# Joining two loads and two stores of a fused RMSNorm-GELU kernel into 64 KB pieces, and gamma into one transfer

## The chip, the cores and the metric

The kernel runs on one core of a Trainium2 chip. The metric is device time in microseconds (us) for one execution, lower is better. A run's profile has its own span, from the first to the last instruction, 1.7 to 2.1 us shorter than the time.

## The reference, cut to what matters

```python
# x: (8, 1024, 2048) float32, gamma: (2048,), eps: 1e-5
rms = np.sqrt(np.mean(x ** 2, axis=-1, keepdims=True) + eps)
out = gamma * x / rms
return 0.5 * out * (1 + np.tanh(np.sqrt(2 / np.pi) * (out + 0.044715 * out ** 3)))
```

x is 67.11 MB and so is the result. Each is moved once.

## The kernel before

The 8192 rows are cut into 16 groups of 512 rows. A group fills one slot: 128 partitions with 4 consecutive rows of 8 KB each, so one partition of a group is a run of 32 KB in memory. There are six slots. Loads are issued by SP ("SPq" in the profile), stores by ACT ("ACTq"). Each is one transfer, except that store 0 is cut into a 64 KB head and the rest.

```python
ROWS = 4; SLOTS = 6; GW = 64; CHUNK = 1024; NARROW = 128
x3 = x.rearrange("b s d -> (b s) d").rearrange("(g p r) d -> g p r d", p=P, r=R)
slot = [sbuf.tile([P, R, D], FP32, name=f"slot{i}") for i in range(SLOTS)]
flat_pieces = {0: [(0, NARROW), (NARROW, R * D)]}

def load(g):
    nc.sync.dma_start(out=slot[g % SLOTS], in_=x3[g])

def gelu_store(g):
    ...                                    # four gelu activations on ACT
    for a, b in flat_pieces.get(g, [(0, R * D)]):
        nc.scalar.dma_start(out=dst[:, a:b], in_=flat[:, a:b])

for k in range(0, D, CHUNK):               # gamma in two transfers
    nc.scalar.dma_start(out=gamma_row[...], in_=gamma[k : k + CHUNK]...)
for g in range(SLOTS):
    load(g)
...                                        # gamma is spread to 128 partitions by matmuls
for g in range(G + 1):
    if g < G:
        squares(...)                       # ACT, 2 or 3 of the 4 rows
        squares_on_vector(...)             # DVE, the others
        inverse_rms(g); scale(g, 0, R)     # DVE, one step on POOL
    if g:
        gelu_store(g - 1)
        if g - 1 + SLOTS < G:
            load(g - 1 + SLOTS)            # waits until store g-1 has left the slot
```

A transfer reports its landing on one of eight completion counters. The build hands these out in turn (not quite in program order: in the changed kernel gamma has counter 0 and load 0 counter 1), so that the eighth transfer gets counter 7 and the ninth counter 0 again.

## Time and profile before

| | before |
|---|---|
| time, first three runs | 317.41 us (317.17 to 317.51) |
| span of the profiled run | 315.3 us |
| busiest compute engines | ACT 66%, DVE 63% |
| DMA, 72 to 300 us | share 1.00, 433 GB/s |
| transfers | 2 gamma + 16 loads + 17 stores = 35 |

The prediction below walks through the page. One part of it that the prediction uses only in numbers is the list of DMA issues (tile, issuer, how many, size of each, median us from issue to landing):

```profile
slot<-in_x_dram SPq DMA_DIRECT2D x16, 4096.0 KB, 31.4
out_dram<-slot ACTq DMA_DIRECT2D x15, 4096.0 KB, 50.0
out_dram<-slot ACTq DMA_DIRECT2D x1, 4032.0 KB, 27.3
out_dram<-slot ACTq DMA_DIRECT2D x1, 64.0 KB, 13.2
```

A 4 MB transfer at 433 GB/s takes 9.7 us alone. That a store takes 50 us to land says that it mostly stands in line.

### The profile page before, as it was taken

The page shows a single profiled execution, that of the slowest core. Times are in us where ns is not written, and L with a number is a line of the kernel's source. Part 1 is how long each engine was busy: PE and PEld are TensorE (multiplying, and loading weights), DVE is VectorE, ACT ScalarE, POOL GpSimd, SP SyncE. Part 2 cuts the span into 40 slices and gives each one's busy share as a digit, 9 for nine tenths or more (in the row PEclk, how much of TensorE's full clock was granted, in tenths as well). Part 3 has the DMA queues.
Part 4 walks back from the last instruction along what each step waited for, and adds up shares of the span by engine and source line. Part 5 has one row for each costly group of instructions (what it writes and reads, how often), then busy time and mean ns, then how long its engine had stood idle before and what let it go on. Part 6 is the DMA issues. An engine that isn't in the chain of part 4 may idle for free.

```text
span 315.3 us, 463 instructions
## 1 busy us (share of the span) xinstructions
PE 7.2 (2%) x8; PEld 2.5 (1%) x8; DVE 198.6 (63%) x129; ACT 207.0 (66%) x150; POOL 16.4 (5%) x21
## 2 busy tenths in 40 slices
PE   0900000000000000000000000000000000000000
PEld 0300000000000000000000000000000000000000
DVE  0089889898988843927687286376934639684000
ACT  1327999999986819569292793948649397499000
POOL 0010110101010101001010010101001010010000
DMA  8999999999999999999999999999999999999996
GB/s 333 412 453 416 452 395 404 461 403 461 417 449 420 442 424 441 420 445 424 441 424 441 428 436 432 432 432 432 432 436 436 428 445 420 453 412 453 412 453 279
DMA packets 4818, 134.24 MB, mean 426 GB/s; under 512 B 592, under 2 KB 720, under 8 KB 720
## 3 DMA queue, kind: packets, MB, share of 16 engines
q1 hardware_dynamic: 2304, 67.11, 49.7%
q10 hardware_dynamic: 2512, 67.12, 49.3%
q14 instruction: 2, 0.02, 0.0%
HBM read 67.12 MB, written 67.11 MB: 426 GB/s over the span
## 4 chain that ended last, share of the span: by engine, by line
another core or an unknown queue 36%; DMA 27%; DVE 16%; ACT 7%; PE 2%; issue 2%; POOL 1%; SPq 1%; ACTq 0%; DVEq 0%; POOLq 0%
DMA out_dram<-slot 14%; DVE slot L109 11%; DMA slot<-in_x_dram 10%; ACT slot L120 7%; DVE spare L82 4%; DMA spare<-in_gamma_dram 2%; PE gamma_ps L142 2%; POOL y L95 1%; SPq L68 1%; ACT junk L72 1%; DVE ms L90 0%; DVE z L98 0%; DVE z L99 0%; DVE rstd L102 0%
## 5 line engine op out<-in xcount | busy, mean ns | idle before, releaser
L109 DVE TENSOR_TENSOR slot<-slot,gamma_ps 128x8192 f32<-128x8192 f32 (+1 forms) x19 | 139.2, 7334 | 0.0
L72 ACT ACTIVATE junk<-slot 128x2048 f32<-128x2048 f32 x42 | 79.0, 1882 | 79.8 <-DMA slot<-in_x_dram 77.4
L120 ACT ACTIVATE slot<-slot,rstd 128x2048 f32<-128x2048 f32 x64 | 122.7, 1987 | 2.8 <-DVE slot L109 2.3
L82 DVE SCALAR_TENSOR_TENSOR spare<-slot 128x2048 f32<-128x2048 f32 x22 | 50.4, 2290 | 43.6 <-DMA slot<-in_x_dram 29.1
L95 POOL TENSOR_TENSOR y<-ms,power 128x4 f32<-128x4 f32 x16 | 16.1, 1007 | 263.1 <-DVE ms L90 263.1
L90 DVE TENSOR_SCALAR ms<-ssq 128x4 f32<-128x4 f32 x16 | 2.7, 170 | 24.2 <-ACT junk L72 22.8
L98 DVE TENSOR_TENSOR z<-ms,y 128x4 f32<-128x4 f32 x16 | 2.6, 164 | 19.0 <-POOL y L95 19.0
L72 ACT ACTIVATION_READ_ACCUMULATOR junk<-slot 128x1 f32 x42 | 7.8, 186 | 0.0
L142 PE MATMUL gamma_ps<-spare,ones 1*128 1x512 f32 x8 | 7.2, 1073 | 8.1 <-DMA spare<-in_gamma_dram 8.1
L102 DVE SCALAR_TENSOR_TENSOR rstd<-z,y 128x4 f32<-128x4 f32 x16 | 2.6, 163 | 0.5
L99 DVE SCALAR_TENSOR_TENSOR z<-z,y 128x4 f32<-128x4 f32 x16 | 2.6, 163 | 0.5
L140 ACT ACT_TABLE_LOAD x1 | 1.3, 1283 | 2.0 <-issue 2.0
L142 PEld LDWEIGHTS gamma_ps<-spare,ones 1*128 1x128 f32 x8 | 2.5, 325 | 11.2 <-issue 10.7
L82 DVE DVE_READ_ACCUMULATOR spare<-slot 128x1 f32 x22 | 1.8, 82 | 0.0
L138 DVE MEMSET warm<- 1x1 f32 x1 | 0.1, 59 | 0.8 <-PEq L181 0.8
L140 ACT ACTIVATE warm<-warm 1x1 f32<-1x1 f32 x1 | 0.2, 202 | 0.0
L139 DVE MEMSET ones<- 1x128 f32 x1 | 0.2, 165 | 0.0
L137 POOL MEMSET power<- 128x4 f32 x1 | 0.1, 101 | 0.3 <-POOLq L181 0.3
L181 POOL MEMSET const-float32-0.0<- 128x1 f32 x1 | 0.1, 98 | 0.2 <-issue 0.2
L181 POOL MEMSET const-bfloat16-1.0<- 128x1 bf16 x1 | 0.1, 102 | 0.0
L181 POOL MEMSET const-uint8-127<- 128x1 uint8 x1 | 0.1, 102 | 0.0
L181 POOL MEMSET const-float32-1.0<- 128x1 f32 x1 | 0.1, 98 | 0.0
## 6 DMA issues: line engine op xcount, KB each, us to landing
slot<-in_x_dram SPq DMA_DIRECT2D x16, 4096.0 KB, 31.4
out_dram<-slot ACTq DMA_DIRECT2D x15, 4096.0 KB, 50.0
out_dram<-slot ACTq DMA_DIRECT2D x1, 4032.0 KB, 27.3
out_dram<-slot ACTq DMA_DIRECT2D x1, 64.0 KB, 13.2
spare<-in_gamma_dram ACTq DMA_DIRECT2D x2, 4.0 KB, 8.2
```

What stands on the lines that cost most here:

```text
L68: nc.sync.dma_start(out=slot[g % SLOTS], in_=x3[g])
L72: nc.scalar.activation(out=junk, in_=slot[g % SLOTS][:, q, :], func=ACT.Square, accum_out=ssq[:, g, q : q + 1],)
L82: nc.vector.scalar_tensor_tensor(out=spare[:, :, 0:GW], in0=row, scalar=1.0, in1=row, op0=ALU.bypass, op1=ALU.mult, accum_out=ssq[:, g, q ...
L90: v.tensor_scalar(out=ms, in0=ssq[:, g, :], scalar1=1.0 / D, scalar2=eps_f, op0=ALU.mult, op1=ALU.add,)
L95: nc.gpsimd.tensor_tensor(out=y_, in0=m_, in1=power, op=ALU.pow)
L98: v.tensor_tensor(out=z_, in0=m_, in1=y_, op=ALU.mult)
L99: v.scalar_tensor_tensor(out=z_, in0=z_, scalar=-0.5, in1=y_, op0=ALU.mult, op1=ALU.mult)
L102: v.scalar_tensor_tensor(out=rstd[:, g, :], in0=z_, scalar=1.5, in1=y_, op0=ALU.add, op1=ALU.mult,)
L109: nc.vector.tensor_tensor(out=rows, in0=rows, in1=gamma_ps.unsqueeze(1).to_broadcast([P, n, D]), op=ALU.mult,)
L120: nc.scalar.activation(out=slot[g % SLOTS][:, r, :], in_=slot[g % SLOTS][:, r, :], func=ACT.Gelu_apprx_tanh, scale=rstd[:, g, r : r + 1],)
L140: nc.scalar.activation(out=warm, in_=warm, func=ACT.Gelu_apprx_tanh)
L142: nc.tensor.matmul(out=gamma_ps[:, k : k + 512], lhsT=ones, rhs=gamma_row[:, k // GW : (k + 512) // GW, 0:GW], start=True, stop=True,)
```

## The change

Its intent is fewer and larger transfers: groups 2 and 3 get 8 consecutive rows per partition and come in one load, 12 and 13 leave in one store, each partition being one run of 64 KB; gamma comes in one transfer. That makes 1 + 15 + 16 = 32 transfers. In the program, gamma's transfer also moves behind the first loads. The core of the diff (cut):

```diff
+LOAD_PAIR = 1
+STORE_PAIR = 6
-GW = 64
-CHUNK = 1024
+GW = 128
+    def pair_part(a, k):
+        n = 2 * R * P
+        return a[k * n : (k + 1) * n].rearrange("(p r) d -> p r d", p=P)
+    def part(a, g):
+        if g // 2 in (LOAD_PAIR, STORE_PAIR):
+            return pair_part(a, g // 2)[:, g % 2 * R : g % 2 * R + R, :]
+        return a[g * R * P : (g + 1) * R * P].rearrange("(p r) d -> p r d", p=P)
...
-    slot = [sbuf.tile([P, R, D], FP32, name=f"slot{i}") for i in range(SLOTS)]
+    pair = [sbuf.tile([P, 2 * R, D], FP32, ...) for i in range(SLOTS // 2)]
+    slot = [pair[i // 2][:, i % 2 * R : i % 2 * R + R, :] for i in range(SLOTS)]
...
+            if g // 2 != STORE_PAIR:
+                nc.scalar.dma_start(out=part(o2, g), in_=slot[g % SLOTS])
+            elif g % 2:
+                nc.scalar.dma_start(
+                    out=pair_part(o2, g // 2), in_=pair[g // 2 % (SLOTS // 2)]
+                )
...
         for g in range(SLOTS):
-            load(g)
+            if g // 2 != LOAD_PAIR:
+                load(g)
+            elif g % 2:
+                nc.sync.dma_start(
+                    out=pair[LOAD_PAIR], in_=pair_part(x2, LOAD_PAIR)
+                )
```

More of the change, by code (lines that the diff above doesn't have):

```diff
@@ L38 @@
     eps_f = float(eps)
-    x3 = x.rearrange("b s d -> (b s) d").rearrange("(g p r) d -> g p r d", p=P, r=R)
-    o3 = out.rearrange("b s d -> (b s) d").rearrange("(g p r) d -> g p r d", p=P, r=R)
-    G = x3.shape[0]
+    x2 = x.rearrange("b s d -> (b s) d")
+    o2 = out.rearrange("b s d -> (b s) d")
+    G = x2.shape[0] // (P * R)
+    def pair_part(a, k):
[5 more added lines that the diff above has]
+        return a[g * R * P : (g + 1) * R * P].rearrange("(p r) d -> p r d", p=P)
     sbuf = ctx.enter_context(tc.tile_pool(name="sbuf", bufs=1))
@@ L46 @@
     )
-    slot = [sbuf.tile([P, R, D], FP32, name=f"slot{i}") for i in range(SLOTS)]
-    spare = sbuf.tile([P, D // GW, GW + 8], FP32, name="spare")
+    pair = [
+        sbuf.tile([P, 2 * R, D], FP32, name=f"pair{i}") for i in range(SLOTS // 2)
+    ]
+    slot = [pair[i // 2][:, i % 2 * R : i % 2 * R + R, :] for i in range(SLOTS)]
+    spare = sbuf.tile([P, D // GW, GW + 16], FP32, name="spare")
     gamma_row = spare[0:1]
@@ L59 @@
     junk = psum.tile([P, D], FP32, name="junk")
-    flat_pieces = {0: [(0, NARROW), (NARROW, R * D)]}
     def on_vector(g):
@@ L67, in load @@
     def load(g):
-        nc.sync.dma_start(out=slot[g % SLOTS], in_=x3[g])
+        nc.sync.dma_start(out=slot[g % SLOTS], in_=part(x2, g))
     def squares(g, r, n):
@@ L114, in scale, with gelu @@
         )
-    def gelu_store(g):
-        flat = slot[g % SLOTS].rearrange("p r d -> p (r d)")
-        dst = o3[g].rearrange("p r d -> p (r d)")
+    def gelu(g):
         for r in range(R):
@@ L125, in gelu_store, with store @@
             )
-        for a, b in flat_pieces.get(g, [(0, R * D)]):
-            nc.scalar.dma_start(out=dst[:, a:b], in_=flat[:, a:b])
-    with tc.manual_schedule():
-        for k in range(0, D, CHUNK):
-            nc.scalar.dma_start(
-                out=gamma_row[:, k // GW : (k + CHUNK) // GW, 0:GW],
-                in_=gamma[k : k + CHUNK].rearrange("(o a b) -> o a b", o=1, b=GW),
-            )
-        for g in range(SLOTS):
-            load(g)
+    def store(g):
+        if g:
+            if g // 2 != STORE_PAIR:
[4 more added lines that the diff above has]
+                )
+            return
+        src = pair[0].rearrange("p r d -> p (r d)")
+        dst = part(o2, 0).rearrange("p r d -> p (r d)")
+        for a, z in ((0, NARROW), (NARROW, R * D)):
+            nc.scalar.dma_start(out=dst[:, a:z], in_=src[:, a:z])
+    with tc.manual_schedule():
+        for g in range(SLOTS):
+            if g // 2 != LOAD_PAIR:
[4 more added lines that the diff above has]
+                )
+        nc.scalar.dma_start(
+            out=gamma_row[:, :, 0:GW],
+            in_=gamma.rearrange("(o a b) -> o a b", o=1, b=GW),
+        )
         nc.gpsimd.memset(power, -0.5)
@@ L161 @@
             if g:
-                gelu_store(g - 1)
+                gelu(g - 1)
+                store(g - 1)
                 if g - 1 + SLOTS < G:
```

## The prediction

> **What bounds the kernel now.** I read the page's engine shares first, then the row of the 40 slices, the table of windows, the waits of the load queue, and last the timeline of the store queue near both ends. The page:
>
> ```profile
> span 315.3 us, 463 instructions
> PE 7.2 (2%) x8; PEld 2.5 (1%) x8; DVE 198.6 (63%) x129; ACT 207.0 (66%) x150; POOL 16.4 (5%) x21
> DMA  8999999999999999999999999999999999999996
> DMA packets 4818, 134.24 MB, mean 426 GB/s; under 512 B 592, under 2 KB 720, under 8 KB 720
> ```
>
> No compute engine is busy more than two thirds of the span, while the DMA row stands at nine tenths from the second slice to the last but one. The 134.24 MB are x read once and the output written once, so no byte can go. How close to a limit the transfers run is seen in windows (start:end, length, five engines' busy time, clock, DMA share, GB/s):
>
> ```profile
> 0.00:5.00 5.00, 0.00 (x0) 0.00 (x0) 0.22 (x2) 1.49 (x2) 0.30 (x5) 1.00 0.75 275
> 2.00:32.00 30.00, 7.16 (x8) 2.48 (x8) 15.32 (x10) 12.92 (x13) 1.01 (x1) 1.00 0.99 426
> 72.00:300.00 228.00, 0.00 (x0) 0.00 (x0) 147.18 (x95) 156.10 (x110) 12.08 (x12) 1.00 1.00 433
> 310.00:315.30 5.30, 0.00 (x0) 0.00 (x0) 0.00 (x0) 0.00 (x0) 0.00 (x0) 1.00 0.47 204
> ```
>
> A DMA share of 1.00 over 228 us at 433 GB/s: the sixteen DMA engines never pause. At 433 GB/s all bytes take 134.24 / 0.433 = 310.0 us. The remaining 5.3 us of the span are its two ends (no byte before 1.5 us; the last leaves at about 312.6 us, its receipt and the program's end take 2.7 us) and a read stage at 426 instead of 433. So **only three things can move the time**: the rate, an emptied queue, or the ends.
>
> The chain of waits puts 36% on "another core or an unknown queue". In order of time these are stretches of 18.9 us between load issues, so I take them for transfer time, as the load queue's own waits say:
>
> ```profile
> SPq L68 <- DMA out_dram<-slot: 223.1, 11, 32.5
> SPq L195 <- DMA out_dram<-slot: 73.4, 1, 73.4
> SPq L68 <- DMA spare<-in_gamma_dram: 5.2, 1, 5.2
> ```
>
> Load g+6 waits until store g has left the slot. Those waits recur every 19.3 us (chain: loads issued at 143.8, 163.2, 182.5 us), and one group's load and store, 8.39 MB, take 8.39 / 0.433 = 19.4 us. The wait is thus the full DMA seen from its issuer.
>
> **What the Trainium skill says.** "DMA: Bandwidth & Descriptors", section "Where 436 GB/s comes from", puts the ceiling of sixteen ports at 435.2 GB/s; the 433 of the trace agrees and leaves 0.5%. Same page, "Why small descriptors are slow (HBM only)": about 3 cycles fixed per packet and 32 B of descriptor data per operation. The trace can't split that, but its 0.5% bounds it. Same page, "Queues, rings and completion order": each engine takes turns between queues packet by packet. The trace fits: the 64 KB store piece (512 B per partition, so 8 packets per engine) took 13.2 us to land beside loads in 32 KB packets, each 32.8 KB / (433/16) = 1.2 us; 8 turns make 9.7 us. Same page, "Anatomy of one DMA": about 2 us fixed per DMA, mostly completion, fitted for the GpSimd path; the queues here are the others, and with several transfers queued nothing of it shows in the 433.
>
> **The change part by part.**
>
> *Fewer transfers.* 35 become 32: 15 loads, 16 stores, 1 gamma. 592 small packets are 35 x 16 completions plus 32 gamma pieces. Afterwards: 32 x 16 = 512, and 16 gamma pieces of 512 B. The two pairs turn 512 pieces of 32 KB into 256 of 64 KB, if nothing splits them. Steady-state loss against 435.2 is 0.5% of 228 us = 1.2 us for 23.5 transfers' worth of bytes, so at most 0.05 us per transfer with all its packets. Three fewer: 0.15 us. The 256 saved packets are 16 per engine; by the page's 3 cycles at its 850 MHz, an estimate of 0.06 us that overlaps with the former. Sum: **0.1 to 0.2 us saved**, 0.05% of the time.
>
> *Gamma in one.* Two issues of 0.60 us on ACT become one; they landed 7.2 to 9.1 us after issue. PE starts its eight matmuls (7.2 us) at 8.08 us when the first lands, and DVE waits for them until 15.3 us. One transfer may start PE within about a microsecond of that either way. This is work that hides: the first full store comes only at 38.3 us, with 25.2 MB of loads queued (58 us). The 5.2 us and 4.7 us in which loads 4 and 5 waited for a transfer counter used by gamma and load 0 fall away (in the build the first five load issues carry no wait), with three loads still queued. Worth 0 us.
>
> *Loads 2 and 3 as one.* Group 2 can't start before both halves are in. At 425 GB/s from 1.8 us, 16.8 MB are through at 41.3 us; load 0 was used 1.2 us after the same reckoning (11.7 against 12.96), so 42.5 us. Before:
>
> ```profile
> 38.28 0.34 ACTq L127 DMA_DIRECT2D out_dram<-slot  x1
> 38.67 1.88 ACT L72 ACTIVATE junk<-slot 128x2048 f32<-128x2048 f32 x1 [0.41 <-ACT slot L120]
> 44.65 7.66 ACT L120 ACTIVATE slot<-slot,rstd 128x2048 f32<-128x2048 f32 x4
> 52.34 0.34 ACTq L127 DMA_DIRECT2D out_dram<-slot  x1
> ```
>
> ACT does the squares of group 2 before the gelu of group 1, so a start at 42.5 instead of 38.67 moves store 1 from 52.3 to **56.2 us** and stores 2 to 4 by the same 4 us. Is the store queue then empty? The main part of store 0 started moving when its 64 KB head had landed (32.6 + 13.2 = 45.8) and landed at 38.28 + 27.3 = 65.6. Now the head first alternates with 64 KB load packets: 3.5 per engine are left at 32.6 us, 2.4 us each, then 4.5 turns of 1.2 us. Done at 46 to 48, so store 0 lands at 66 to 68. Store 1 at 56.2 is still 10 us early; and loads 4 and 5 are queued anyhow. Later, store 5 waited for load 6: store 4 was issued at 93.2, store 5 at 109.1, but the ACT work between is 4.0 + 7.7 us, leaving some 4 us of idle time that absorbs the delay. Worth 0 us at the end.
>
> *Stores 12 and 13 as one.* Store 12 now leaves with store 13:
>
> ```profile
> 246.91 0.34 ACTq L127 DMA_DIRECT2D out_dram<-slot  x1
> 266.24 0.34 ACTq L127 DMA_DIRECT2D out_dram<-slot  x1
> 283.58 0.34 ACTq L127 DMA_DIRECT2D out_dram<-slot  x1
> 291.73 0.34 ACTq L127 DMA_DIRECT2D out_dram<-slot  x1
> ```
>
> These are stores 12 to 15. Store 12 goes out 19.3 us later. Store 9 landed at 240.5 (it released load 15), store 10 by the 19.4 us rhythm at 259.9. Store 11 then shares with load 15 until that lands at 271.9 (12 us at half rate, 2.6 MB) and needs (4.2 - 2.6) / 0.433 = 3.7 us more: 275.6 us. The pair at 266.2 is queued **9 us before it is needed**. It then takes 19.4 us, to 295, and stores 14 and 15 (283.6, 291.7) are both queued by then. No slot waits for stores 12 and 13, as no load follows. Worth 0 us.
>
> Sum: 317.41 - 0.15, about **317.2 us**.
>
> **The rivals.** (1) *The queue runs dry.* For it: two joined transfers hold back work for 4 and 19 us. Against it: margins of 10 and 9 us, and a load beside each. Should the end lag by all it could, say the pair leaving 12 us later, it would cost 3 us: about 320. (2) *64 KB pieces run at another rate.* They are 16.8 of 134.2 MB. 10% slower would cost 16.8 / 0.433 x 0.1 = 3.9 us, 321. Nothing in the profile shows a piece of that size, so I can't exclude it, but 32 KB pieces already reach 433 of 435.2, so faster gains little. (3) *The per-transfer cost is larger than bounded here*, because the read stage at 426 hides some: 7 GB/s over 30 us is 0.5 us for three loads, or 0.16 us each, so three fewer give 0.5 us: 316.9. (4) *Turns between queues become unequal*: a 64 KB packet against 32 KB ones takes two thirds. It only shifts bytes between directions, and the pair store meets no load after 275.6 us. 317.2.
>
> **Range and chances.** The three runs before span 0.34 us. I add half a microsecond either way for another phase of reads against writes, and a little on the slow side for rivals 1 and 2: 316.5 to 318.3. Faster by over 2% would be 311.1 us; with all bytes at the page's 435.2 GB/s (308.5 us) and ends of 1.5 and 2.7 us plus the 2.1 us between span and time, it is 314.8, so hardly possible: 1%. Slower by over 2% is 323.8, which takes a rate loss of a sixth in the 64 KB pieces or an idle DMA of 6 us: 3%.
>
> **What would show it.** DMA row still nines; 433 in the middle; packets 4498 with 512 under 512 B (4754 if pieces are split); store 1 near 56 us; load 6 at 66 to 68 us; the pair store near 266 us; last issue near 292 us; last bytes near 312.5. A slice under nine tenths after 40 or after 266 us would speak for rival 1; fewer GB/s around 22 to 42 or 276 to 295 us for rival 2.

## The result, and the profile after

Six runs of the changed kernel have a median of **316.95 us** (316.77 to 317.22), six of the kernel before 317.46 us (317.17 to 317.75). The ratio is 0.9985, with a 95% interval from 0.9972 to 0.9998. The change is worth half a microsecond by the medians: within 2%, and just clear of no change at all, since the interval allows 0.06 to 0.9 us.

The page of the changed kernel:

```profile
span 315.1 us, 457 instructions
...
DMA  8999989999999999999999999999999999999896
...
DMA packets 4498, 134.24 MB, mean 426 GB/s; under 512 B 512, under 2 KB 656, under 8 KB 656
```

The packet counts are the ones worked out ahead (4498 and 512), so the 64 KB pieces go whole. Two slices of the DMA row stand at 8, at 39 to 47 and 292 to 299 us. The prediction had named such slices as the sign of an emptied queue, so they must be read with care. The windows (start:end, length, busy time of five engines, clock, DMA share, GB/s) over the first of them, and the long middle:

```profile
22.00:42.00 20.00, 0.00 (x0) 0.00 (x0) 18.64 (x9) 13.68 (x10) 1.01 (x1) 1.00 1.00 434
32.00:52.00 20.00, 0.00 (x0) 0.00 (x0) 14.89 (x14) 16.21 (x13) 2.02 (x2) 1.00 0.93 386
...
72.00:300.00 228.00, 0.00 (x0) 0.00 (x0) 149.64 (x96) 158.88 (x114) 12.08 (x12) 1.00 1.00 434
...
1.50:2.00 0.50, 0.00 (x0) 0.00 (x0) 0.00 (x0) 0.50 (x1) 0.00 (x0) 1.00 2.99 786
```

The second of these stretches before the change:

```profile
32.00:52.00 20.00, 0.00 (x0) 0.00 (x0) 17.28 (x14) 19.52 (x14) 2.02 (x2) 1.00 0.99 412
```

The line from 1.50 to 2.00 us gives it away: no engine can be busy 2.99 times over. The view books a packet, with all its time and bytes, at the moment it starts. A 64 KB piece lasts 2.4 us and sixteen of them start together, so a slice can lack a whole row of them. When I spread each packet record of the trace over its own duration, every stretch of 10 us from 10 to 310 us is busy to 1.00, in both kernels. The eights are bookkeeping; nothing idles. The windows from 22 to 42 and from 276 to 295 us, which the prediction had named for rival 2, read 434 and 426 GB/s (433 and 428 before); spread in the same way both move 434, so the 64 KB pieces are no slower.

The DMA issues: single loads, the rest and the head of store 0, gamma, and the two joined transfers (8 MB, printed without a size):

```profile
pair<-in_x_dram SPq DMA_DIRECT2D x14, 4096.0 KB, 25.5
...
out_dram<-pair ACTq DMA_DIRECT2D x1, 4032.0 KB, 31.3
out_dram<-pair ACTq DMA_DIRECT2D x1, 64.0 KB, 17.6
spare<-in_gamma_dram ACTq DMA_DIRECT2D x1, 8.0 KB, 7.4
pair<-in_x_dram SPq DMA_DIRECT2D x1, 40.5
out_dram<-pair ACTq DMA_DIRECT2D x1, 30.9
```

And the timeline of ACT: the first squares of group 2, store 1, the joined store, the last store.

```profile
42.16 1.88 ACT L87 ACTIVATE junk<-pair 128x2048 f32<-128x2048 f32 x1 [3.72 <-DMA pair<-in_x_dram]
...
55.83 0.34 ACTq L143 DMA_DIRECT2D out_dram<-pair  x1
...
264.01 0.34 ACTq L145 DMA_DIRECT2D out_dram<-pair  x1
...
289.38 0.34 ACTq L143 DMA_DIRECT2D out_dram<-pair  x1
```

ACT now waits 3.72 us for the joined load, and store 1 leaves at 55.8 instead of 52.3 us. The joined store is issued at 264.0 us and lands 30.9 us later, at 294.9. As its 8.39 MB take 19.4 us, it began to move at about 275.5 us: it stood in line for 11 us.

The remaining difference is at the very end. The load queue's last waits are those of the program's end (source line 195 before, 225 after). Before, one wait of 73.4 us, shown in the prediction; after:

```profile
SPq L225 <- DMA out_dram<-pair: 44.5, 4, 19.3
SPq L225 <- DMA pair<-in_x_dram: 25.1, 1, 25.1
```

Before, the end sits in one wait until everything has landed. After, it moves from one landing to the next, and only the last is left when the last bytes land. Why that is worth time is told with the last experiment.

### The profile page after: what moved, and what is told of

Its sections match the earlier page's. It is cut to its first block, busy times and chain, and to the rows that moved or that the text cites. A ratio compares the mean times of both kernels' runs of the same rounds, so it can differ in the third digit from the quotient of the medians. Undisturbed runs are those within 1.5% of the kernel's fastest.

```text
span 315.1 us, 457 instructions
## 1 busy us (share of the span) xinstructions
PE 7.2 (2%) x8; PEld 2.5 (1%) x8; DVE 198.5 (63%) x129; ACT 206.9 (66%) x150; POOL 16.4 (5%) x21
## 2 busy tenths in 40 slices
DMA packets 4498, 134.24 MB, mean 426 GB/s; under 512 B 512, under 2 KB 656, under 8 KB 656
## 3 DMA queue, kind: packets, MB, share of 16 engines
q10 hardware_dynamic: 2336, 67.12, 49.3%
## 4 chain that ended last, share of the span: by engine, by line
another core or an unknown queue 36%; DMA 36%; ACT 18%; issue 1%; SPq 1%; ACTq 0%
DMA pair<-in_x_dram 21%; DMA out_dram<-pair 15%; ACT pair L133 12%; ACT junk L87 6%; SPq L83 1%; ACTq L143 0%
## 5 line engine op out<-in xcount | busy, mean ns | idle before, releaser
L124 DVE TENSOR_TENSOR pair<-pair,gamma_ps 128x8192 f32<-128x8192 f32 (+1 forms) x19 | 139.2, 7334 | 0.0
L87 ACT ACTIVATE junk<-pair 128x2048 f32<-128x2048 f32 x42 | 79.0, 1881 | 78.7 <-DMA pair<-in_x_dram 76.2
L133 ACT ACTIVATE pair<-pair,rstd 128x2048 f32<-128x2048 f32 x64 | 122.6, 1987 | 2.3 <-DVE pair L124 1.9
L97 DVE SCALAR_TENSOR_TENSOR spare<-pair 128x2048 f32<-128x2048 f32 x22 | 50.4, 2291 | 39.3 <-DMA pair<-in_x_dram 24.6
L87 ACT ACTIVATION_READ_ACCUMULATOR junk<-pair 128x1 f32 x42 | 7.8, 186 | 0.0
L97 DVE DVE_READ_ACCUMULATOR spare<-pair 128x1 f32 x22 | 1.8, 83 | 0.0
## 6 DMA issues: line engine op xcount, KB each, us to landing
out_dram<-pair ACTq DMA_DIRECT2D x1, 64.0 KB, 17.6
out_dram<-pair ACTq DMA_DIRECT2D x1, 30.9
```

Source lines behind the costliest of these rows:

```text
L87: nc.scalar.activation(out=junk, in_=slot[g % SLOTS][:, q, :], func=ACT.Square, accum_out=ssq[:, g, q : q + 1],)
L97: nc.vector.scalar_tensor_tensor(out=spare[:, :, 0:GW], in0=row, scalar=1.0, in1=row, op0=ALU.bypass, op1=ALU.mult, accum_out=ssq[:, g, q ...
L124: nc.vector.tensor_tensor(out=rows, in0=rows, in1=gamma_ps.unsqueeze(1).to_broadcast([P, n, D]), op=ALU.mult,)
L133: nc.scalar.activation(out=slot[g % SLOTS][:, r, :], in_=slot[g % SLOTS][:, r, :], func=ACT.Gelu_apprx_tanh, scale=rstd[:, g, r : r + 1],)
```

## The experiments

Twelve kernels ran, all correct. The diffs below are cut, and those of e8 and e11 put more simply than they were made. My theory: the DMA engines are the bound, fewer pieces and transfers save some tenths of a microsecond, and holding back groups 2 and 12 costs nothing because other transfers stand in line. The rivals: the gain comes from one part alone; the held-back work costs something that the rest pays for; pieces or transfers have quite another price.

| run | transfers, last counter | median us (runs) | ratio to before, 95% interval | last landing to end of span, us |
|---|---|---|---|---|
| before (first six) | 35, third | 317.46 (6) | | 1.04 |
| the change | 32, last | 316.95 (6) | 0.9985 (0.9972 to 0.9998) | 0.82 |
| e1 gamma in one | 34, second | 317.34 (5) | 1.0002 (0.9989 to 1.0014) | 0.98 |
| e2 load pair | 34, second | 317.25 (5) | 0.9997 (0.9985 to 1.0010) | 0.98 |
| e3 store pair | 34, second | 317.13 (5) | 1.0001 (0.9988 to 1.0013) | 0.98 |
| e4 the change again | 32, last | 316.98 (5) | 0.9983 (0.9970 to 0.9997) | 0.82 |
| e5 8 KB pieces | 35, third | 320.45 (4) | 1.0091 (1.0073 to 1.0109) | 1.04 |
| e6 16 KB pieces | 35, third | 318.77 (4) | 1.0036 (1.0020 to 1.0053) | 1.04 |
| e7 16 KB, two each | 65, first | 319.45 (4) | 1.0054 (1.0036 to 1.0073) | 0.93 |
| e8 no head | 31, seventh | 319.01 (4) | 1.0037 (1.0014 to 1.0061) | 0.89 |
| e9 load pair 0, 1 | 32, last | 318.03 (4) | 1.0015 (0.9995 to 1.0035) | 0.82 |
| e10 store pair 14, 15 | 32, last | 317.12 (4) | 0.9985 (0.9968 to 1.0002) | 0.82 |
| e11 all pairs | 17, first | 346.88 (4) | 1.0923 (1.0903 to 1.0944) | 0.92 |
| e12 joins, 35 transfers | 35, third | 317.09 (5) | 0.9990 (0.9976 to 1.0004) | 1.05 |

The last column is worked out from the trace: the span less the moment at which the last store's counter reaches its full count.

### The parts alone, and the whole again (e1 to e4)

e1 is the kernel before with the gamma part of the diff; e2 and e3 are the changed kernel with gamma in two again and one pair switched off:

```diff
-STORE_PAIR = 6        # e2: the load pair alone
+STORE_PAIR = -1
-LOAD_PAIR = 1         # e3: the store pair alone
+LOAD_PAIR = -1
```

> Only the gamma part of the change on the kernel before (one transfer of 8 KB in 512 B pieces, the loads ahead of it in the program). Theory (the DMA engines are the bound; a transfer less saves its completion packet, some 9 ns per engine, and ACT's second issue no longer meets the first load's): 0.1 us faster at most, 317.3 to 317.5, first load issue shorter than 0.64 us, PE start near 8.3 us. Rival (all of the measured half microsecond comes from gamma's place at the start): 0.4 to 0.5 us faster, about 317.0.

> Only the joined load of groups 2 and 3; gamma and the stores as before. Theory: the 64 KB pieces save 8 pieces per engine at about 8 ns, 0.06 us; store 1 moves to near 55.8 us and nothing idles: 317.35 to 317.45. Rival (the joined load costs, by holding group 2 back): slower by up to 1 us and a slice of the DMA row under nine tenths after 40 us.

> Only the joined store of groups 12 and 13; gamma and the loads as before. Theory: 0.06 us faster, 317.35 to 317.45; the pair store is issued near 266 us and no slice after it falls under nine tenths before the last one. Rival (64 KB pieces leave the store queue faster, or the held-back store empties it): more than 0.4 us either way.

> The changed kernel again, beside its parts on the same chip. Theory: the parts add up to 0.2 to 0.3 us and the half microsecond measured first was partly spread: 317.1 to 317.3 if before is 317.45. Rival (a real half microsecond that the parts do not explain): 316.95 again, ratio 0.9985 with an interval clear of 1.

Measured beside a median of 317.38 us for the kernel before: 317.34, 317.25, 317.13, and 316.98 for the whole. No part alone has an interval clear of 1, the whole has one again. My expectation for e4 (317.1 to 317.3) was wrong: the gain is real, though its size is known no better than the two intervals say (0.06 to 0.9 and 0.1 to 0.95 us). By medians the parts give 0.04 + 0.13 + 0.25 = 0.42 us, close to the whole's 0.40, but by the ratios of the table (1.0002, 0.9997, 1.0001) they give nothing, and each is of the size of the spread of runs (317.00 to 317.95 in e3 alone). So these runs show no split. In e2 store 1 leaves at 56.0 us (55.8 in the changed kernel), and in e3 the joined store at 266.4; neither is slower. The eight in the DMA row at 39 to 47 us is there in e2, the one at 292 to 299 us in e3: each goes with its own 64 KB stage.

### The price of a piece and of a transfer (e5 to e7)

The saving was too small to be measured directly, so these runs add pieces and transfers by the hundred. e5 and e6 deal the rows of a group so that a partition's share lies in four or two separate runs; e7 issues each half of e6 by itself. Group 0 is left as it was.

```diff
-        return rows.rearrange("(p r) d -> p r d", p=P)
+        return rows.rearrange("(h p r) d -> p h r d", h=4, p=P)   # e5; h=2 in e6, e7
...
+        for h in range(2):                                        # e7, loads and stores
+            nc.sync.dma_start(out=tile_part(g)[:, h], in_=part(x2, g)[:, h])
```

> Kernel before with the rows of groups 1 to 15 dealt so that each partition moves four pieces of 8 KB instead of one of 32 KB, the same 35 transfers. This adds 15 groups x 2 directions x 8 partitions x 3 = 720 pieces per engine. Theory by the packet records of before and after (a 64 KB piece takes 2418 ns, two of 32 KB take 2 x 1213, so 8 ns per piece): 720 x 8 ns = 5.8 us slower, about 323.2. Rival by the skill's 3 cycles per packet at 850 MHz, 3.5 ns: 2.5 us slower, about 320. Rival (pieces of this size cost nothing, only transfers do): 317.5.

> As the 8 KB kernel, with two pieces of 16 KB: 240 pieces more per engine. Theory: 240 x 8 ns = 1.9 us slower, about 319.4. Rival (3.5 ns each): 0.8 us, 318.3. Rival (no cost of pieces): 317.5.

> The 16 KB kernel with each load and store of groups 1 to 15 issued as two transfers of one half each: 30 transfers more, the same pieces. Theory (a transfer costs its completion packets, some 9 ns per engine, while others are queued): 30 x 9 ns = 0.3 us slower than the 16 KB kernel, about 319.7. Rival (each transfer costs 0.05 to 0.16 us as the prediction's bounds allow): 1.5 to 5 us slower. Rival (about 2 us fixed per transfer shows): 60 us. Caution: with eight completion counters in rotation the stores may wait for older ones, which would show as a DMA row under nine tenths.

The kernel before had a median of 317.44 us in these rounds. e5: 3.01 us for 720 pieces per engine, **4.2 ns a piece** (3.2 to 4.8 by the interval). e6: 1.33 us for 240, 5.5 ns (2.6 to 7). My figure of 8 ns, read from packet records (1213 ns for 32 KB, 2418 for 64 KB), was too high, by half to double: e5 came out near its rival's 320 (the estimate from the 3 cycles of "DMA: Bandwidth & Descriptors" that the prediction cites), not at my 323.2. Dealing the rows also changes where in memory a partition's pieces lie; no run tells that apart from their number. The records themselves add up to more than the time that passed: in e5 the packet time per engine sums to 317.9 us, while 315.5 us lie between the first byte and the last, so packets of the two queues overlap a little, and part of each packet's fixed cost is hidden. e7 is 0.68 us slower than e6, though its end is 0.11 us shorter: 0.8 us for 30 transfers, 0.026 us each (up to about 0.05 by the two intervals). Part of that may not be the transfers' own price: in e7 one store went out 19 us after its data were ready, and its second half 10 us after that, for want of a counter, and one slice near the end shows 367 GB/s.

For the change this means: 16 pieces per engine fewer, 0.07 to 0.13 us (4.2 to 8 ns each), and three transfers, 0.08 us (at most 0.15 by the intervals).

### The head of store 0 (e8)

```diff
-        for a, z in ((0, NARROW), (NARROW, R * D)):
-            nc.scalar.dma_start(out=dst[:, a:z], in_=src[:, a:z])
+        nc.scalar.dma_start(out=part(o2, 0), in_=slot[0])
```

> The changed kernel with store 0 in one transfer, without its 64 KB head: 31 transfers. The packet records of both kernels show 0.7 us of slow 32 KB pieces between 37 and 47 us, when the head passes. Theory (it is the head's 512 B pieces between reads): the slow pieces vanish and the time falls by 0.5 to 0.7 us, to about 316.4. Rival (it is the first writes of any kind): no change, 316.95 within 0.2.

A miss: 319.01 us, two microseconds slower than the change. The slow pieces near 40 us are still there (0.9 us per engine, from 38 to 43 us), so they are no work of the head. In the changed kernel they are 32 KB reads that start between 46 and 48 us, when the head's last pieces pass and the first large write is about to start (49.3 us). The loss shows at the end: of the last sixteen pieces in the trace, one row of the sixteen engines, eleven end by 313.6 us, the others at 313.9, 314.4, 314.7, 314.7 and 315.88. With the head, in the changed kernel, all sixteen end between 313.0 and 313.9. Without it the engines come out less level, and the last of them sets the time. That this is what the head is for, and how it would do it, these runs don't show.

### Other places for the joins (e9, e10)

```diff
-LOAD_PAIR = 1
+LOAD_PAIR = 0          # e9
-STORE_PAIR = 6
+STORE_PAIR = 7         # e10
```

> The changed kernel with the joined load at groups 0 and 1 instead of 2 and 3. Group 0 then starts near 22.5 us instead of 13 us, and store 0 leaves some 8 us later, near 46 us. Theory (only an emptied queue costs, and the six first loads fill it until about 60 us): no change, 316.7 to 317.3. Rival (the start of the first store sets the end): up to 8 us slower, 325.

> The changed kernel with the joined store at groups 14 and 15 instead of 12 and 13: store 14 is held back until group 15 is done. Theory: the pair leaves near 289.5 us, stores 12 and 13 keep the engines busy until about 293 to 295 us, so 3 to 5 us are to spare: no change, 316.7 to 317.4. Rival (the margin is counted wrong and the queue empties): up to 10 us slower, with a slice near 285 to 295 us under nine tenths.

e10 went as expected: the joined store leaves at 288.1 us, later than any store but the last before, and the time is 317.12 us. Its margin was larger than expected: store 13 landed at 295.3 us, so the pair stood in line for 7 us, and that was enough. A margin of 3 to 5 us was not tried. e9 came out at 318.03, 0.7 us over the range I gave, though far from the rival's 8 us. The packet records sum to 0.44 us more per engine than the changed kernel's, and the last byte leaves 0.70 us later. About 0.3 us of it are slow pieces between 70 and 100 us, after a stretch (70 to 80 us) in which only 21% of the packet time were reads: the first six loads were through, and load 6 had just begun. The DMA engines were never idle (1.00 in every stretch of 10 us from 10 to 310 us), so the theory that only an emptied queue costs is wrong by this 0.7 us. An uneven mix of the two queues goes with the slow pieces here; that it causes them was not tested, and the rest of the loss is unexplained.

### All joined (e11)

```diff
-        nc.sync.dma_start(out=slot[g % SLOTS], in_=part(x2, g))
+        if g % 2:
+            nc.sync.dma_start(
+                out=pair[g // 2 % (SLOTS // 2)], in_=pair_part(x2, g // 2)
+            )                       # and the same for the stores
```

> Every load and every store joined, three double slots, 17 transfers. Theory (fewer transfers gain 0.008 us per piece and 0.009 us per completion, 1 us at most; but now the queue must run dry): a load waits for a whole pair store to land, so 1 to 2 us idle in each of five turns, and at the end the last pair's 8.4 MB can leave only when group 15 is done, some 34 us after its load landed: 10 to 17 us slower, 328 to 336, with slices under nine tenths in the last fifth. Rival (fewer and larger transfers are what gains): faster than 316.95 by 1 to 2 us.

346.88 us: the direction is the theory's, the size nearly double. The DMA row of this kernel's page:

```profile
DMA  9989898988989979989699998999898898089897
```

Two of its windows near the end:

```profile
296.00:303.00 7.00, 0.00 (x0) 0.00 (x0) 6.13 (x4) 6.98 (x4) 0.76 (x1) 1.00 0.00 0
303.00:323.00 20.00, 0.00 (x0) 0.00 (x0) 16.82 (x13) 19.24 (x12) 1.01 (x1) 1.00 0.97 419
```

Here the zero in the row is real: from 296 to 303 us nothing moves while ACT works through a pair whose store can't leave before both groups are done. Spread over their durations, the packets leave 2.0 to 2.3 us idle at each of the five turns where a load waits for a whole pair to land, 10.7 us in all, and 10.5 us from 293 to 303 us. Most of the rest of the 29.5 us are slow pieces: 10.3 us per engine above the usual duration, against 1.4 in the kernel before, nearly all of them reads that start within some 10 us after a turn. I had counted the idle turns and the end, not the slow pieces. This is what rival 1 of the prediction looks like when it happens, and it separates the two effects: fewer pieces and transfers (17 instead of 35) bring nothing when the queue runs dry.

### The end of the program (e12)

By now pieces and transfers explained 0.1 to 0.2 of the half microsecond. The table's last column shows another part: the time from the last landing to the end has only five values, to within 0.01 us, and they follow the counter of the last store alone. The built program shows why. Its end is a row of waits on SP, in this order:

```
wait counters 2 and 3
wait counters 1 and 4
wait counters 0 and 5
wait counter 6 (and PE)
wait counter 7 (and ACT)
```

Before, transfer 35 falls on the third counter (number 2): the first of these waits holds until the last landing, and four more have to be gone through after it. With 32 transfers the last store falls on counter 7, and nothing but its own wait is left. (In the profile, too, the instructions of SP after the last landing start 0.06 us apart.) The steps are 1.04, 0.98, 0.93, 0.89 and 0.82 us, about 0.055 us a wait.

e12 keeps both joins but cuts gamma into four, ahead of the loads, so that there are 35 transfers again:

```diff
+        for k in range(0, D, 512):
+            nc.scalar.dma_start(
+                out=gamma_row[:, k // GW : (k + 512) // GW, 0:GW],
+                in_=gamma[k : k + 512].rearrange("(o a b) -> o a b", o=1, b=GW),
+            )
```

> Both joins in 64 KB pieces as in the changed kernel, but gamma in four transfers ahead of the loads, so that there are 35 transfers again and the last store falls on the third of the eight completion counters, as before, instead of on the last of them. In all traces so far the time from the last landing to the end of the span follows that counter alone: 1.04 us for the third, 0.98 to 0.99 for the second, 0.82 for the last. Theory (0.22 us of the gain is this end, 0.15 us the saved pieces and completions): the end takes 1.04 us, and the time is 317.2, 0.2 to 0.25 below before. Rival (the gain is the 64 KB pieces alone): 316.95 to 317.0. Rival (the gain is the single gamma transfer at the start): 317.4.

```profile
SPq L226 <- DMA out_dram<-pair: 69.7, 1, 69.7
```

The single long wait is back, and the end takes 1.05 us. So the 0.22 us at the end are shown: all thirteen traces taken before this run fit the counter, and here the length was foretold. The four small gamma transfers bring no more completion packets than the one did (4498 packets in both pages), so e12 keeps all that the change saves in packets and differs from it in gamma's start and in the end. The time, 317.09 us beside 317.51 for the kernel before, lies between the theory and the rival: its interval (0.9976 to 1.0004) does not tell 317.2 from 317.0. The length of the end is thus shown in the traces, but not its share of the time.

## Why the prediction was right or wrong

The range (316.5 to 318.3) and the class (no difference of 2%) were right; the point, 317.2, was 0.25 us too high by the medians, which the runs hardly resolve: the foretold gain of 0.15 us lies in both intervals. By its steps:

- **The bound**: right. The DMA engines are busy to 1.00 in both kernels, and taking up to 20 us of time from a store's issue (store 12, or store 14's 7 us in e10) cost nothing that the times show.
- **Fewer transfers, 0.1 to 0.2 us**: right in size for what it named. The packet records of the profiled runs sum to 312.35 us per engine before and 312.21 after; by the prices of e5 to e7 it is 0.07 to 0.2 us. The 3 cycles per packet of "DMA: Bandwidth & Descriptors" in the Trainium skill (section "Why small descriptors are slow (HBM only)"), at its 850 MHz an estimate of 3.5 ns, are close to the measured 4.2.
- **Gamma, 0 us**: right within the spread (e1: 317.34 beside 317.38). PE started at 8.27 us instead of 8.08, and the later work didn't mind.
- **Loads 2 and 3**: right. The data were used at 42.2 us (42.5 foretold), store 1 left at 55.8 (56.2). Store 0 landed at 69.7 us, not 66 to 68: its head took 17.6 us instead of 13 to 15. The engines did give the head one piece between two load pieces, as foretold; what the sum left out is that its first piece starts only 3.4 us after its issue (3.7 before). Load 6 followed that, without any effect.
- **Stores 12 and 13**: right. Landing 294.9 us (295 foretold), issue 264.0 (266.2), last issue 289.4 (292), and 11 us of margin instead of 9.
- **The sum, where the miss lies**: "its receipt and the program's end take 2.7 us" was held to be the same before and after. That term was not looked into. First, it was misread: packets are booked at their start, so the last byte left at 313.9 us, not 312.6, and receipt and end take 1.4 us (0.34 us to the landing, 1.04 after it). Second, it is not constant: the waits at the end shrink from 1.04 to 0.82 us because 32 is a multiple of eight. In the profiled pair it is all that changed: the last byte leaves at 313.92 us before and at 313.93 after. (One pair can't show the 0.1 to 0.2 us of the pieces: in e4, the same kernel again, it leaves at 314.20.) Together with those 0.1 to 0.2 us the account comes to 0.3 to 0.4 us, and that fits the spans (recorded to 0.1 us), whose medians are 315.5 us before (28 runs) and 315.2 for the change (11 runs). The remaining 0.14 us of the measured half microsecond lie outside the span: the time is on average 1.93 us longer than the span before (1.79 to 2.10), and 1.79 for the change (1.76 to 1.83). No trace covers that stretch, and its cause stays open.
- **Rival 1** is what e11 became; **rival 2** was untrue (64 KB pieces ran at 27.1 GB/s per engine, 32 KB ones at 27.0); **rival 3** had the best number, 316.9, for a reason that e7 excludes (0.026 us per transfer, 0.05 at most by the intervals, not 0.16).

I didn't find a version that beats both kernels; e8 to e11 were the candidates.

## What to carry to other kernels

When transfers fill the whole span, ask of each held-back transfer how long it would have stood in line anyway: that margin, read from issue-to-landing times, says whether joining is free, and e11 shows the cost when it is not. Piece and transfer counts are worth nanoseconds once pieces are 32 KB; to price such things, multiply them by hundreds instead of removing three. Look at what the program does after the last landing too, for a few waits left there (0.22 us in the traces) weighed more here than the large pieces (0.07 to 0.13 us by the price of a piece).

## What the Trainium skill lacked or had wrong

- "DMA: Bandwidth & Descriptors", section "Queues, rings and completion order": it lets an engine drain a packet of about 9 to 17 descriptors before it turns to the other queue. Here the turn was one piece: the 8 pieces of 512 B per engine of store 0's head start 1.2 us apart beside 32 KB pieces and up to 2.5 us apart beside 64 KB ones, one for each piece of the loads, and the head took 13.2 and 17.6 us to land.
- Same page, "Anatomy of one DMA": the 2 us fixed per transfer are fitted for the GpSimd path; it gives no price for a transfer issued by SP or ACT into a full queue. e7 puts it at 0.026 us, at most about 0.05.
- No page that I read has the order of the waits at a program's end: 0.055 us for each wait left after the last landing, up to 0.22 us.
- No page that I read says that read pieces run slower for a while when loads start, or when stores start beside them: 0.6 to 0.7 us per engine in the first 3 us and 0.7 us at 43 to 48 us in both kernels, 10.3 us in all in e11, mostly after its turns. Why, these runs don't show.
